# Loading the expert weights of a decoder layer in 2 MB transfers instead of 1 MB ones

## The chip, the cores and the metric

The kernel runs on one core of one Trainium2 chip. The metric is the device time of one execution in microseconds (us). TensorE (PE) multiplies matrices, VectorE (DVE), ScalarE (ACT) and GpSimd (POOL) work on elements, and SyncE (SP) issues nearly all loads; an issued load is moved by the core's 16 DMA engines, which write into the on-chip memory (SBUF, 128 partitions). All numbers are fp32.

## The reference, cut to what matters

The layer has a token mixer (sparse attention beside an RWKV-7 recurrence) and then a mixture of 32 experts over 256 tokens, of which each token uses two. Only the second part bears on the change. Each expert has three weight matrices of 2 MB: gate and up (1024 x 512) and down (512 x 1024).

```python
def body(acc, ew):
    wg, wu, wd, cw = ew
    hdn = jax.nn.silu(xt @ wg) * (xt @ wu)
    return acc + cw[:, None] * (hdn @ wd).astype(f32), None

acc, _ = lax.scan(body, jnp.zeros((T, D), f32), (w_gate, w_up, w_down, combine.T))
```

All 32 experts' weights are read, 192 MB in all, whatever the routing is: for each expert the kernel gathers up to 32 tokens, and a loop at the end, which runs only where an expert has more, takes the rest.

## The kernel before, in words

The first part of the layer takes some 350 us. The experts then go in eight quads of four (`for q in range(NQ)`). For a quad, the tokens are gathered into 128 columns (`fetch`), 32 for each expert. `rows_in` multiplies them with the gate weights and then with the up weights of the four experts: one matmul fills 32 of the 128 rows of a PSUM bank, so four experts run beside each other, and the row blocks `k` of the weights are summed over. `hidden` and `turn_hidden` make silu(gate) x up and transpose it, `rows_down` multiplies with the down weights, `times_gate` and `finish` scale the result and add it to four accumulators in the next quad. The last quad is written out apart (`cols_down`, `parts_down`, `leave`), so that the first 512 columns of the output can leave while the second 512 are computed.

The loads stand in one list, in the order in which they are issued. A weight matrix is cut into two halves of 1 MB: `("eg", e, 0)` and `("eg", e, 1)` are the first and second four row blocks of expert e's gate weights, of which each partition holds a run of 8 KB; `eu` and `ed` are the up and down weights. In the last quad the down weights are cut by columns instead (`ENDS`), and a partition's 1 MB share then comes in four runs of 2 KB. The very first quad's first gate halves come as four `row` loads over four experts.

`pump` issues the next loads of the list as long as the allocator (`Arena`) finds room, in the arena and then in the pool called more, which is the space that an earlier stage has left. `need` gives a loaded tile to the matmuls, and `done` gives its room back and calls `pump`. All this happens when the program is built: the order on SP's queue is the order of the list, and a load into room that has been used waits on the chip for the last matmul that read the tile before it. The loads also take turns on eight completion semaphores, and one that takes a semaphore waits until the load eight places before it, which had the same one, has landed.

In the built program of before, the 1 MB loads of the later quads go round 20 places. A gate group of a quad is 16 matmuls for the first halves of four experts and 16 for the second, each matmul of two instructions (fp32); each half's places are freed after its own 16 matmuls. The names and lines that follow: L288 issues the loads, L1626 is `rows_in`, L1653 `rows_down`, L1660 `cols_down`, L1666 `parts_down`, L1708 `finish`, L1611 the gather.

Of the kernel before, what the change touches and what calls it, by code (L numbers as in the profile page):

```python
# [63 lines left out]
LORD = (0, 1, 2, 3, 4, 5, 6, 7, 8, 9, 10, 12, 13, 15, 11, 14, 17, 16, 18, 23, 19, 20, 21, 22, 24, 28, 25, 27, 26, 29, 30, 31, 32, 33, 34, 35, 36, 37, 38, 44, 40, 39, 41, 42, 51, 45, 43, 47, 48, 52, 50, 46, 49)  # L64
INFO = []
QUADS = NE // 4
ENDS = ((0, 512), (512, 512))
ADAE = 'PPDDDDDDDDDDDDDDDPPPPPPDPPPDPPPDPPPDDDDDDDDDDDDDDDDDDDPPPPPPPPPP'
ADAP = 4
# [88 lines left out]
def layer_kernel(tc, I, out, dbg=None):  # L158
    nc = tc.nc
# [35 lines left out]
    def PS(tag=None):  # L195
        tag = tag or state["tag"]
        return psp.tile([128, 512], F32, name="ps_" + tag, tag=tag, bufs=NB[tag])
# [6 lines left out]
    def add_load(key, shape, parts):  # L204
        loads.append((key, shape, parts))
# [55 lines left out]
    for k in range(4):  # L261
        add_load(("row", k), (1, 2048), [((512 * e, 512 * e + 512), I["expert_w_gate"][0, e].rearrange("(p k) n -> p k n", p=128)
                                          [:, k:k + 1, :]) for e in range(4)])
    for q in range(QUADS):
        for n, name, r in (("eg", "expert_w_gate", 4), ("eu", "expert_w_up", 4), ("ed", "expert_w_down", 2)):
            for i, (c, m) in enumerate(ENDS if n == "ed" and q == QUADS - 1 else ((0, None), (0, None))):
                for e in range(4 * q, 4 * q + 4 if q or n != "eg" or i else 0):
                    w = I[name][0, e].rearrange("(p k) n -> p k n", p=128)
                    if m is None:
                        add_load((n, e, i), (r, 2048 // r), [(None, w[:, r * i:r * i + r, :])])  # L270
                    else:
                        add_load((n, e, i), (4, m), [(None, w[:, :, c:c + m])])
# [20 lines left out]
    def need(key):  # L293
        assert key in W, ("not loaded", key, list(W))
        return W[key]

    def done(key, then=None):
        t = W.pop(key)
        next(a for a in [A] + state["more"] if id(t) in a.live).free(t)
        if then is not None:  # L300
            then()
        pump()
# [90 lines left out]
    for k2 in range(4):  # L393
        ps = PS("rrra"[k2])
# [27 lines left out]
    def mod_bcast(o, row, g0, mul):  # L422

        for g in range(2):
            ps = PS()
            q = 32 * (g0 + g)
            nc.tensor.matmul(ps, ident[:, q:q + 1].to_broadcast([128, 128]), row, start=True, stop=True)
            nc.scalar.mul(o[:, 512 * g:512 * g + 512], ps, mul)
# [69 lines left out]
    def step(it, keep):  # L498

        return after_last(lambda: next(it, "end"), keep)  # L500
# [918 lines left out]
    while todo:  # L1419
# [11 lines left out]
        n = min(turn, key=PRIO.index)  # L1431
# [7 lines left out]
        c = step(it, FORCE)  # L1439
# [53 lines left out]
    for j in range(4):  # L1493
        w = need(("wo", j))
        ws = {}
# [34 lines left out]
    def ME(*shape, dtype=None):  # L1530
        return next(ap for ap in (a.get(*shape, dtype=dtype) for a in [A] + state["more"]) if ap is not None)
# [89 lines left out]

    def rows_in(ps, xg, ws, i):

        for k in range(4):
            for g, w in enumerate(ws):
                nc.tensor.matmul(ps[32 * g:32 * g + 32, :], xg[:, 4 * i + k, 32 * g:32 * g + 32], w[:, k, :],  # L1626
                                 start=(i == 0 and k == 0), stop=(i == 1 and k == 3))

    def row_in(ps, xg, w, k):

        for g in range(4):
            nc.tensor.matmul(ps[32 * g:32 * g + 32, :], xg[:, k, 32 * g:32 * g + 32], w[:, 0, 512 * g:512 * g + 512],  # L1632
                             start=(k == 0), stop=False)

    def hidden(psg, psu, r):

        nc.scalar.activation(thb[0:r], psg[0:r, :], AF.Tanh, scale=0.5)  # L1637
        nc.vector.scalar_tensor_tensor(thb[0:r], thb[0:r], 1.0, psg[0:r, :], op0=OP.add, op1=OP.mult)  # L1638
        nc.vector.scalar_tensor_tensor(hidb[0:r].rearrange("p (j q) -> p q j", j=4), thb[0:r].rearrange("p (q j) -> p q j", j=4),  # L1639
                                       0.5, psu[0:r, :].rearrange("p (q j) -> p q j", j=4), op0=OP.mult, op1=OP.mult)  # L1640

    def turn_hidden(r):
        ps = PS()
        for j in range(4):
            nc.tensor.transpose(ps[:, r * j:r * j + r], hidb[0:r, 128 * j:128 * j + 128], ident[0:r, 0:r])
        nc.scalar.copy(hTb[:, :, 0:r], ps[:, 0:4 * r].rearrange("p (j s) -> p j s", j=4))

    def rows_down(pss, ws, i):

        for c in range(2):  # L1650
            for j in range(2):
                for g, w in enumerate(ws):
                    nc.tensor.matmul(pss[c][32 * g:32 * g + 32, :], hTb[:, 2 * i + j, 32 * g:32 * g + 32],  # L1653
                                     w[:, j, 512 * c:512 * c + 512], start=(i == 0 and j == 0), stop=(i == 1 and j == 1))

    def cols_down(ps, ws):

# [19 lines left out]
    def places(q):  # L1677

        full = [128, 2, 4, CAP]
        es = slice(4 * q, 4 * q + 4)  # L1680
        nc.vector.tensor_tensor(eqb, io1[:, None, None, :].to_broadcast(full), rk[:, :, es][:, :, :, None].to_broadcast(full),
                                op=OP.is_equal)
        for a in range(2):
            nc.vector.tensor_scalar(OHb[:, a], eqb[:, a], rs2[:, a:a + 1], None, op0=OP.mult)

    def fetch(q, k2s=range(4)):
        gather(XGb[q % 2], lambda a: OHb[:, a], 128, k2s)

    def scatter(q):

        nc.gpsimd.tensor_mul(o4b, eqb, comb[:, :, 4 * q:4 * q + 4][:, :, :, None].to_broadcast([128, 2, 4, CAP]))  # L1691
        ps = PS()
        for a in range(2):
            nc.tensor.transpose(ps[:, 128 * a:128 * a + 128], o4b[:, a].rearrange("p g s -> p (g s)"), ident)  # L1694
        nc.scalar.copy(stb[q % 2], ps[:, 0:256].rearrange("p (a t) -> p a t", a=2))

    def begin():

        for a in range(2):
            for c in range(2):  # L1700
                nc.tensor.matmul(acc[2 * a + c].rearrange("p (c k) -> p c k", k=8), ident,  # L1701
                                 h2[:, a, :, 64 * c:64 * c + 64].rearrange("p k c -> p c k"), start=True, stop=False)

    def finish(st, c, r=128, o=None, stop=False):

        o = c if o is None else o
        for a in range(2):
            nc.tensor.matmul(acc[2 * a + c // 512], st[0:r, a, :], Yb[0:r, o:o + 512], start=False, stop=stop)  # L1708
# [12 lines left out]
    def late_rows():  # L1721
# [2 lines left out]

    thb = hidb = hTb = stb = Yb = None
    late = {("eu", 0, 1): late_hidden, ("eu", 1, 1): lambda: (gt2.append(ME(1024)), XGb.append(ME(8, 128))),
            ("eu", 2, 1): late_rows, ("eu", 11, 1): late_tables}
    places(0)
    NQ = QUADS
    for q in range(NQ):  # L1730
        es = range(4 * q, 4 * q + 4)
        psg, psu = PS(), PS()
        for n, ps in (("eg", psg), ("eu", psu)):
            for i in range(2):
                if q == 0 and n == "eg":
                    for k2 in range(2 * i, 2 * i + 2):
                        fetch(0, [k2])
                        for k in () if i else (2 * k2, 2 * k2 + 1):
                            row_in(ps, XGb[0], need(("row", k)), k)
                            done(("row", k))  # L1740
                    if i == 0:
                        continue
                rows_in(ps, XGb[q % 2], [need((n, e, i)) for e in es], i)
                for e in es:
                    done((n, e, i), late.get((n, e, i)))
        hidden(psg, psu, 128)
        if q == 0:
            begin()
            scatter(0)
        if q:  # L1750
            for c in (0, 512):
                finish(stb[(q - 1) % 2], c)
        else:
            mod_bcast(gt2[0], row2, 2, 1.0)
            A.free(row2)
        if q == NQ - 1:
            break
        places(q + 1)
        fetch(q + 1)
        scatter(q + 1)  # L1760
        if q == 2:
            overflow_tables(nc, ovm, PS(), sel, rk, comb, ones, io)
        turn_hidden(128)
        pss = [PS(), PS()]
        for i in range(2):
            rows_down(pss, [need(("ed", e, i)) for e in es], i)
            for e in es:
                done(("ed", e, i))
        for c in range(2):
            times_gate(512 * c, pss[c])  # L1770
# [6 lines left out]
    ps = PS()  # L1777
# [18 lines left out]
    ps = PS()  # L1796
# [4 lines left out]
    ps, p4 = PS(), PS()  # L1801
# [14 lines left out]
    with tc.If(nov > 0):  # L1816
# [3 lines left out]
        with tc.For_i(0, nov, 1) as i:  # L1820
# [15 lines left out]
            for c in (0, 512):  # L1836
                ps = PS()
                parts_down(ps, 0, wts[2][:, :, c:c + 512])
                times_gate(c, ps)
            ps = PS()  # L1840
# [5 lines left out]
            for a in range(2):  # L1846
                for c in range(2):
                    ps = PS()
# [104 lines left out]
```

## Time and profile before

| | us |
|---|---|
| median of 3 runs | 796.88 (796.73 to 797.54) |
| the profiled execution | 798.72 |
| its span, first to last instruction | 796.8 |
| TensorE busy in the span | 676.4 (85%) |
| VectorE, ScalarE, GpSimd busy | 285.3, 167.6, 144.2 |

The span is shown in 40 slices of 19.92 us. Each slice has a digit for the busy share of an engine and of the 16 DMA engines, and the GB/s that these moved. The chain of waits follows the last instruction back to what released it, and so on to the start. A packet is one run of bytes that one DMA engine moves. "SPq" is SP's queue of issues: a load's own time there is the issuing alone, not the transfer.

### The profile page before, as it was taken

To read this page: it belongs to the slowest core of one execution; us is meant where nothing else is said; L and a number is where in the kernel's file an instruction comes from. 1 tells how busy PE (TensorE), PEld (TensorE's weight loads), DVE (VectorE), ACT (ScalarE), POOL (GpSimd) and SP (SyncE) were. 2 spreads that over 40 slices of the span, in tenths; PEclk is the share of its full clock that TensorE was granted. 3 is DMA by queue.
4 is the path that set the end of the run, shared out by engine and by line. 5 is a ranking of instruction groups with operands and counts; after the bars stand their busy time and mean duration, and the time that the engine had idled before them with its cause. 6 is when DMAs were issued, how large, how long until landed. Compare 5 with 4: busy or idle time off the path is not lost.

```text
span 796.8 us, 11470 instructions
## 1 busy us (share of the span) xinstructions
PE 676.4 (85%) x4657; PEld 364.7 (46%) x4657; DVE 285.3 (36%) x665; ACT 167.6 (21%) x347; POOL 144.2 (18%) x176
## 2 busy tenths in 40 slices
PE   5897989799998998889999778878768868878667
PEld 2785657468888877853342312312312312312112
DVE  2577789697336557741210160100100100100001
ACT  2445412144156644321110100100100100000000
POOL 1446744331314117610000000000000000000000
PEclk9899999899999999989999899899999999899889
DMA  9997467443656456779999999999999999999994
GB/s 333 389 308 253 165 221 282 146 154 105 218 208 239 133 178 246 292 257 420 422 421 422 421 420 422 421 420 423 420 421 422 420 421 422 420 421 422 422 392 180
DMA packets 63590, 261.38 MB, mean 328 GB/s; under 512 B 7952, under 2 KB 19216, under 8 KB 38448
## 3 DMA queue, kind: packets, MB, share of 16 engines
q1 hardware_dynamic: 63248, 260.11, 83.4%
q8 instruction: 37, 0.61, 0.3%
q10 hardware_dynamic: 288, 0.52, 0.2%
q14 instruction: 17, 0.14, 0.0%
HBM read 259.57 MB, written 1.05 MB: 327 GB/s over the span
## 4 chain that ended last, share of the span: by engine, by line
DMA 46%; PE 10%; DVE 3%; SPq 1%; issue 1%; POOL 1%; ACT 0%; POOLq 0%; DVEq 0%
DMA arena<-in_expert_w_down_dram 17%; DMA arena<-in_expert_w_gate_dram 13%; DMA arena<-in_expert_w_up_dram 12%; DMA more<-in_expert_w_gate_dram 2%; DMA more<-in_expert_w_up_dram 2%; PE ps_e L1626 2%; DVE split L520 1%; PE ps_e L1611 1%; SPq L288 1%; PE ps_e L1660 1%; PE acc L1701 1%; PE acc L1708 1%; PE ps_e L1653 1%; PE ps_e L1632 0%; PE ps_r L1471 0%
## 5 line engine op out<-in xcount | busy, mean ns | idle before, releaser
L1626 PE MATMUL ps_e<-arena,more 128*32 128x512 f32 x440 | 87.6, 656 | 23.9 <-DMA arena<-in_expert_w_gate_dram 12.0
L1626 PE MATMUL ps_e<-arena 128*32 128x512 f32 x416 | 82.4, 682 | 20.4 <-DMA arena<-in_expert_w_gate_dram 11.7
L1653 PE MATMUL ps_e<-arena 128*32 128x512 f32 x360 | 84.3, 609 | 13.5 <-DMA arena<-in_expert_w_down_dram 9.6
L520 DVE TENSOR_TENSOR split<-arena,split 128x512 fp32r<-128x512 f32 x77 | 70.7, 928 | 45.6 <-ACT split L519 31.8
L1637 ACT ACTIVATE arena<-ps_e 128x512 f32<-128x512 f32 x8 | 4.8, 597 | 244.8 <-PE ps_e L1626 244.8
L1638 DVE SCALAR_TENSOR_TENSOR arena<-arena,ps_e 128x512 f32<-128x512 f32 x8 | 5.5, 688 | 140.2 <-ACT arena L1637 140.2
L1691 POOL TENSOR_TENSOR arena<-arena 128x256 f32<-128x256 f32 x8 | 4.9, 615 | 280.7 <-PE ps_e L1694 279.0
L1670 DVE TENSOR_TENSOR arena<-ps_e,more 128x512 f32<-128x512 f32 (+1 forms) x17 | 11.8, 691 | 122.2 <-PE ps_e L1653 109.1
L519 ACT CAST split<-arena 128x512 fp32r<-128x512 f32 x66 | 45.0, 688 | 48.1 <-PE ps_g L531 30.3
L520 POOL TENSOR_TENSOR split<-arena,split 128x512 fp32r<-128x512 f32 x33 | 47.2, 1431 | 42.6 <-ACT split L519 27.8
L564 PE MATMUL ps_a<-split 128*128 128x256 f32 x360 | 52.1, 304 | 3.1 <-ACT split L476 1.9
L1626 PEld LDWEIGHTS ps_e<-arena,more 128*32 128x32 f32 x440 | 19.4, 118 | 76.3 <-issue 30.9
L564 PEld LDWEIGHTS ps_a<-split 128*128 128x128 f32 x360 | 47.9, 205 | 12.1 <-issue 6.5
L1626 PEld LDWEIGHTS ps_e<-arena 128*32 128x32 f32 x416 | 17.8, 122 | 74.0 <-issue 35.8
L517 POOL TENSOR_SCALAR split<-arena 128x512 fp32r<-128x512 f32 x44 | 36.9, 842 | 70.2 <-PE ps_g L531 18.7
L1653 PEld LDWEIGHTS ps_e<-arena 128*32 128x32 f32 x360 | 19.6, 110 | 64.3 <-issue 31.2
L530 PE MATMUL ps_g<-split 128*128 128x256 f32 x128 | 39.1, 306 | 0.0
L532 PE MATMUL ps_g<-split 128*128 128x256 f32 x128 | 36.9, 289 | 2.0 <-POOL split L520 2.0
L1639 DVE SCALAR_TENSOR_TENSOR arena<-arena,ps_e 128x512 f32<-128x512 f32 x8 | 8.2, 1029 | 82.5 <-PE ps_e L1626 82.5
L531 PE MATMUL ps_g<-split 128*128 128x256 f32 x128 | 36.8, 288 | 0.0
L1611 PEld LDWEIGHTS ps_e<-arena,more 128*128 128x128 f32 x256 | 30.7, 195 | 13.2 <-issue 8.2
L532 PE MATMUL ps_a<-split 128*128 128x256 f32 (+1 forms) x96 | 30.4, 317 | 6.2 <-DVE split L520 6.2
(378 smaller groups left out, 1192.5 us busy)
## 6 DMA issues: line engine op xcount, KB each, us to landing
arena<-in_expert_w_gate_dram SPq DMA_DIRECT2D x54, 1024.0 KB, 19.8
arena<-in_expert_w_up_dram SPq DMA_DIRECT2D x53, 1024.0 KB, 19.8
arena<-in_expert_w_down_dram SPq DMA_DIRECT2D x53, 1024.0 KB, 19.8
arena<-in_w_in_dram SPq DMA_DIRECT2D x18, 1024.0 KB, 7.8
arena<-in_ada_w_dram SPq DMA_DIRECT2D x16, 1024.0 KB, 6.1
more<-in_expert_w_up_dram SPq DMA_DIRECT2D x11, 1024.0 KB, 19.8
more<-in_expert_w_down_dram SPq DMA_DIRECT2D x11, 1024.0 KB, 19.8
arena<-in_ada_w_dram SPq DMA_DIRECT2D x16, 512.0 KB, 10.9
```

Of the source, the lines that this page charges most:

```text
L517: nc.gpsimd.tensor_scalar(h, w, 1.0, 0.0, op0=OP.mult, op1=OP.add)
L519: nc.scalar.copy(h, w)
L520: (nc.gpsimd if p[1] == "P" else nc.vector).tensor_sub(l, w, h.bitcast(F32))
L530: nc.tensor.matmul(ps, l[0], r[0], start=start, stop=False)
L531: nc.tensor.matmul(ps, l[0], r[1], start=False, stop=False)
L532: nc.tensor.matmul(ps, l[1], r[0], start=False, stop=stop)
L564: nc.tensor.matmul(p, a[:, kk, :], b[:, 4 * hf + kk, :], start=(i == 0 and kk == KORD[0]), stop=(i == 2 and kk == KORD[-1]))
L1611: nc.tensor.matmul(ps[:, n * kk:n * kk + n], h2[:, a, 2 * k2 + kk, :], oh(a), start=(a == 0), stop=(a == 1))
L1626: nc.tensor.matmul(ps[32 * g:32 * g + 32, :], xg[:, 4 * i + k, 32 * g:32 * g + 32], w[:, k, :], start=(i == 0 and k == 0), stop=(i == 1 an ...
L1639: nc.vector.scalar_tensor_tensor(hidb[0:r].rearrange("p (j q) -> p q j", j=4), thb[0:r].rearrange("p (q j) -> p q j", j=4), 0.5, psu[0:r, ...
L1653: nc.tensor.matmul(pss[c][32 * g:32 * g + 32, :], hTb[:, 2 * i + j, 32 * g:32 * g + 32], w[:, j, 512 * c:512 * c + 512], start=(i == 0 and ...
L1670: nc.vector.tensor_mul(Yb[0:r, c:c + 512], ps[0:r], gt2[0][0:r, g:g + 512])
```

## The change

From the third quad on, that is from expert 8, a weight matrix comes in one load of 2 MB: the four row blocks twice over, 16 KB in one run for each partition. The up and down weights of the last quad keep their 1 MB pieces, the down weights their column halves. `rows_in` and `rows_down` take as many row blocks as the tile has, so that one call covers what two covered, and the loops over the two halves run once. The room for the overflow tables is taken when the one up tile of expert 11 is freed.

```diff
--- before.py
+++ after.py
@@ -64,6 +64,7 @@
 LORD = (0, 1, 2, 3, 4, 5, 6, 7, 8, 9, 10, 12, 13, 15, 11, 14, 17, 16, 18, 23, 19, 20, 21, 22, 24, 28, 25, 27, 26, 29, 30, 31, 32, 33, 34, 35, 36, 37, 38, 44, 40, 39, 41, 42, 51, 45, 43, 47, 48, 52, 50, 46, 49)
 INFO = []
 QUADS = NE // 4
+WHOLE = 2
 ENDS = ((0, 512), (512, 512))
 ADAE = 'PPDDDDDDDDDDDDDDDPPPPPPDPPPDPPPDPPPDDDDDDDDDDDDDDDDDDDPPPPPPPPPP'
 ADAP = 4
@@ -261,9 +262,18 @@
     for k in range(4):
         add_load(("row", k), (1, 2048), [((512 * e, 512 * e + 512), I["expert_w_gate"][0, e].rearrange("(p k) n -> p k n", p=128)
                                           [:, k:k + 1, :]) for e in range(4)])
+    def whole(n, q):
+
+        return q >= WHOLE and not (n != "eg" and q == QUADS - 1)
+
     for q in range(QUADS):
         for n, name, r in (("eg", "expert_w_gate", 4), ("eu", "expert_w_up", 4), ("ed", "expert_w_down", 2)):
             for i, (c, m) in enumerate(ENDS if n == "ed" and q == QUADS - 1 else ((0, None), (0, None))):
+                if whole(n, q):
+                    if i == 0:
+                        for e in range(4 * q, 4 * q + 4):
+                            add_load((n, e, 0), (2 * r, 2048 // r), [(None, I[name][0, e].rearrange("(p k) n -> p k n", p=128))])
+                    continue
                 for e in range(4 * q, 4 * q + 4 if q or n != "eg" or i else 0):
                     w = I[name][0, e].rearrange("(p k) n -> p k n", p=128)
                     if m is None:
@@ -1621,10 +1631,10 @@
 
     def rows_in(ps, xg, ws, i):
 
-        for k in range(4):
+        for k in range(4 * i, 4 * i + ws[0].shape[1]):
             for g, w in enumerate(ws):
-                nc.tensor.matmul(ps[32 * g:32 * g + 32, :], xg[:, 4 * i + k, 32 * g:32 * g + 32], w[:, k, :],
-                                 start=(i == 0 and k == 0), stop=(i == 1 and k == 3))
+                nc.tensor.matmul(ps[32 * g:32 * g + 32, :], xg[:, k, 32 * g:32 * g + 32], w[:, k - 4 * i, :],
+                                 start=(k == 0), stop=(k == 7))
 
     def row_in(ps, xg, w, k):
 
@@ -1648,10 +1658,10 @@
     def rows_down(pss, ws, i):
 
         for c in range(2):
-            for j in range(2):
+            for j in range(2 * i, 2 * i + ws[0].shape[1]):
                 for g, w in enumerate(ws):
-                    nc.tensor.matmul(pss[c][32 * g:32 * g + 32, :], hTb[:, 2 * i + j, 32 * g:32 * g + 32],
-                                     w[:, j, 512 * c:512 * c + 512], start=(i == 0 and j == 0), stop=(i == 1 and j == 1))
+                    nc.tensor.matmul(pss[c][32 * g:32 * g + 32, :], hTb[:, j, 32 * g:32 * g + 32],
+                                     w[:, j - 2 * i, 512 * c:512 * c + 512], start=(j == 0), stop=(j == 3))
 
     def cols_down(ps, ws):
 
@@ -1724,14 +1734,14 @@
 
     thb = hidb = hTb = stb = Yb = None
     late = {("eu", 0, 1): late_hidden, ("eu", 1, 1): lambda: (gt2.append(ME(1024)), XGb.append(ME(8, 128))),
-            ("eu", 2, 1): late_rows, ("eu", 11, 1): late_tables}
+            ("eu", 2, 1): late_rows, ("eu", 11, 0 if whole("eu", 2) else 1): late_tables}
     places(0)
     NQ = QUADS
     for q in range(NQ):
         es = range(4 * q, 4 * q + 4)
         psg, psu = PS(), PS()
         for n, ps in (("eg", psg), ("eu", psu)):
-            for i in range(2):
+            for i in range(1 if whole(n, q) else 2):
                 if q == 0 and n == "eg":
                     for k2 in range(2 * i, 2 * i + 2):
                         fetch(0, [k2])
@@ -1762,7 +1772,7 @@
             overflow_tables(nc, ovm, PS(), sel, rk, comb, ones, io)
         turn_hidden(128)
         pss = [PS(), PS()]
-        for i in range(2):
+        for i in range(1 if whole("ed", q) else 2):
             rows_down(pss, [need(("ed", e, i)) for e in es], i)
             for e in es:
                 done(("ed", e, i))
```

On SP's queue, at the change from the second quad to the third (L288 before is L298 now):

```order
L288 DMA arena<-in_expert_w_down_dram 128x2048 x6
L288 DMA arena<-in_expert_w_gate_dram 128x2048 x8
L288 DMA arena<-in_expert_w_up_dram 128x2048 x3
L288 DMA more<-in_expert_w_up_dram 128x2048 x3
L288 DMA arena<-in_expert_w_up_dram 128x2048 x2
L288 DMA arena<-in_expert_w_down_dram 128x2048 x8
```

Now:

```order
L298 DMA arena<-in_expert_w_down_dram 128x2048 x6
L298 DMA arena<-in_expert_w_gate_dram 128x4096 x4
L298 DMA more<-in_expert_w_up_dram 128x4096
L298 DMA arena<-in_expert_w_up_dram 128x4096 x3
L298 DMA arena<-in_expert_w_down_dram 128x4096 x4
L298 DMA more<-in_expert_w_gate_dram 128x4096
```

Eight gate loads of 1 MB become four of 2 MB, and the up and down loads behind them likewise; the tiles' places differ, one of four being in more. In all, 128 loads of 1 MB become 64 of 2 MB. In the built program these go round eight places of 2 MB, two sets of four.

On TensorE, at the third quad's gate matmuls (L1626 before is L1636 now, L1708 is L1718, L1611 is L1621, L1694 is L1704):

```order
L1708 MATMUL acc_3382<-arena 128x512
L1708 MATMUL acc_3384<-arena 128x512
L1626 MATMUL ps_e<-arena 32x512
L1708 MATMUL acc_3383<-arena 128x512
L1708 MATMUL acc_3385<-arena 128x512
L1626 MATMUL ps_e<-arena 32x512 x32
L1611 MATMUL ps_e<-arena,more 128x128 x11
L1626 MATMUL ps_e<-arena 32x512
L1611 MATMUL ps_e<-arena,more 128x128 x5
L1694 MATMUL ps_e<-arena 128x128 x2
```

Now:

```order
L1718 MATMUL acc_3382<-arena 128x512
L1718 MATMUL acc_3384<-arena 128x512
L1718 MATMUL acc_3383<-arena 128x512
L1718 MATMUL acc_3385<-arena 128x512
L1636 MATMUL ps_e<-arena 32x512 x32
L1636 MATMUL ps_e<-more,arena 32x512
L1621 MATMUL ps_e<-arena,more 128x128 x13
L1636 MATMUL ps_e<-arena 32x512
L1621 MATMUL ps_e<-arena,more 128x128 x3
L1704 MATMUL ps_e<-arena 128x128 x2
```

The first gate matmul stood among the four `finish` matmuls and waited for the first gate half; now the four stand together, and the 32 gate matmuls of the quad follow in one piece. The count of matmuls is as before. `rows_down` runs over all four row blocks for the first 512 columns and then for the second, where it ran over two blocks for both. VectorE's, ScalarE's and GpSimd's orders are the same in both programs.

On SP's queue, the last quad's loads:

```order
L288 DMA arena<-in_expert_w_gate_dram 128x2048 x8
L288 DMA arena<-in_expert_w_up_dram 128x2048 x3
L288 DMA more<-in_expert_w_up_dram 128x2048 x3
L288 DMA arena<-in_expert_w_up_dram 128x2048 x2
L288 DMA arena<-in_expert_w_down_dram 128x4x512 x8
```

Now:

```order
L298 DMA more<-in_expert_w_gate_dram 128x4096
L298 DMA arena<-in_expert_w_gate_dram 128x4096 x3
L298 DMA arena<-in_expert_w_up_dram 128x2048 x2
L298 DMA more<-in_expert_w_up_dram 128x2048
L298 DMA arena<-in_expert_w_up_dram 128x2048 x5
L298 DMA arena<-in_expert_w_down_dram 128x4x512 x3
L298 DMA more<-in_expert_w_down_dram 128x4x512 x2
L298 DMA arena<-in_expert_w_down_dram 128x4x512 x3
```

The first two rows now are the 2 MB gate loads; behind them stand eight up loads and eight down column halves of 1 MB in both programs, in other places.

## Rows read from the trace of the kernel before

**Rows 1.** The page's slices: DMA busy share, GB/s moved, and the packets by size

```profile
DMA  9997467443656456779999999999999999999994
GB/s 333 389 308 253 165 221 282 146 154 105 218 208 239 133 178 246 292 257 420 422 421 422 421 420 422 421 420 423 420 421 422 420 421 422 420 421 422 422 392 180
DMA packets 63590, 261.38 MB, mean 328 GB/s; under 512 B 7952, under 2 KB 19216, under 8 KB 38448
```

**Rows 2.** The page's chain that ended last: shares of the span by engine, then by line

```profile
DMA 46%; PE 10%; DVE 3%; SPq 1%; issue 1%; POOL 1%; ACT 0%; POOLq 0%; DVEq 0%
DMA arena<-in_expert_w_down_dram 17%; DMA arena<-in_expert_w_gate_dram 13%; DMA arena<-in_expert_w_up_dram 12%; DMA more<-in_expert_w_gate_dram 2%; DMA more<-in_expert_w_up_dram 2%; PE ps_e L1626 2%; DVE split L520 1%; PE ps_e L1611 1%; SPq L288 1%; PE ps_e L1660 1%; PE acc L1701 1%; PE acc L1708 1%; PE ps_e L1653 1%; PE ps_e L1632 0%; PE ps_r L1471 0%
```

**Rows 3.** Chain in order of time, from 713 us: start us, us, what

```profile
713.16 19.78 DMA arena<-in_expert_w_gate_dram
733.01 19.81 DMA arena<-in_expert_w_up_dram
752.88 9.20 SPq L288
762.17 13.97 DMA arena<-in_expert_w_down_dram
776.18 5.14 PE ps_e L1660 x26
...
784.07 3.25 PE ps_e L1660 x21
...
788.61 3.65 PE acc L1708 x8
```

**Rows 4.** Stretches: columns as the first row names them, the last two are DMA share, GB/s

```profile
core 0: us, PE busy (x) PEld busy (x) DVE busy (x) ACT busy (x) POOL busy (x), PEclk, DMA share, GB/s
...
520.00:740.00 220.00, 174.36 (x854) 50.88 (x854) 17.13 (x32) 9.75 (x22) 2.83 (x4) 0.96 1.01 421
764.00:778.00 14.00, 9.36 (x50) 2.67 (x54) 1.02 (x1) 0.86 (x2) 0.00 (x0) 0.80 1.05 387
```

**Rows 5.** The page's DMA issues: form xcount, KB each, us from issue to landing

```profile
arena<-in_expert_w_gate_dram SPq DMA_DIRECT2D x54, 1024.0 KB, 19.8
arena<-in_expert_w_up_dram SPq DMA_DIRECT2D x53, 1024.0 KB, 19.8
```

**Rows 6.** Line 288 (all loads): issue to landing, shortest, median, longest

```profile
DMA to landing us min/median/max: 2.8/19.8/21.4
```

**Rows 7.** Waits of SP's queue: us in total, times, longest us

```profile
SPq L288 <- DMA arena<-in_expert_w_gate_dram: 93.9, 45, 2.1
SPq L288 <- DMA arena<-in_expert_w_up_dram: 86.7, 42, 2.2
...
SPq L288 <- PE ps_e L1653: 15.2, 13, 9.4
...
SPq L288 <- PE ps_e L1626: 11.3, 18, 4.5
```

**Rows 8.** Order of time on SP's queue, 406 to 449 us: start us, us, what

```profile
406.91 19.29 SPq L288 DMA_DIRECT2D arena<-in_expert_w_gate_dram  x8
428.36 5.30 SPq L288 DMA_DIRECT2D arena<-in_expert_w_up_dram  x3
435.81 5.28 SPq L288 DMA_DIRECT2D more<-in_expert_w_up_dram  x3
```

**Rows 9.** Order of time on TensorE, 729 to 752 us: start us, us, what [idle before]

```profile
729.08 1.98 PE L1708 MATMUL acc<-arena 128*128 128x512 f32 x4
...
735.46 3.63 PE L1626 MATMUL ps_e<-arena,more 128*32 128x512 f32 x28 [0.53 <-DMA arena<-in_expert_w_gate_dram]
740.43 1.05 PE L1626 MATMUL ps_e<-arena,more 128*32 128x512 f32 x2 [1.34 <-DMA arena<-in_expert_w_gate_dram]
742.92 1.05 PE L1626 MATMUL ps_e<-arena,more 128*32 128x512 f32 x2 [1.44 <-DMA arena<-in_expert_w_gate_dram]
745.41 6.02 PE L1626 MATMUL ps_e<-arena,more 128*32 128x512 f32 x30 [1.44 <-DMA arena<-in_expert_w_gate_dram]
```

## The prediction

> **What bounds the kernel now.** I read the page's slices first: from the 19th on, some 360 us into the span, the DMA engines are busy 9 tenths or more and move 420 to 423 GB/s slice after slice, to the 38th [rows 1]. Before that the digits are mostly lower and the time goes to the token mixer. Then the chain of waits: 46% of the span on it is DMA and 10% TensorE, and the DMA is nearly all expert weights [rows 2]. In order of time it shows blocks of eight 1 MB loads of about 19.8 us each, one behind the other, until the last down pieces land at 776.18 us, then the last quad's matmuls and the output [rows 3]. So the second half of the kernel is a stream at a steady rate: its length is bytes by rate, and it is followed by a tail of some 20 us.
>
> The stream is not starved. A load takes 19.8 us from issue to landing, where one takes 2.49 us of the engines (below), so eight are in flight [rows 5]. SP waits longest in total for earlier loads, in steps of at most 2.2 us, that is for one of the eight semaphores; its waits for matmuls to free room sum to 15.2 and 11.3 us over the whole span [rows 7], and in the stretch from 520 to 740 us the engines stand at a share of 1.01 in spite of them [rows 4]. TensorE is busy 174.36 of those 220 us, some of it at a lower clock (0.96 on the mean) [rows 4]; it waits for the loads.
>
> So the change matters through the rate of the stream, through the risk that bigger places starve it, and through the tail.
>
> **The rate.** Two stretches are pure in the size of their runs. From 520 to 740 us every partition's share is a run of 8 KB, and the rate is 421 GB/s; from 764 to 778 us the last quad's down pieces come in runs of 2 KB, and it is 387 GB/s [rows 4]. 1 MB (1,048,576 bytes) takes 2.491 us in the first and 2.709 us in the second. Each of 16 engines moves 64 KB of it, in 8 runs or in 32. The difference, 218 ns over 24 more runs, is 9.1 ns a run; without runs' cost 1 MB would take 2.491 - 8 x 0.0091 = 2.418 us, which is 434 GB/s. That a run of 8 KB is one packet is borne out by the count: 63,590 - 38,448 = 25,142 packets are of 8 KB or more [rows 1]; 180 expert loads and 16 others with such runs make 196 x 128 = 25,088.
>
> With 16 KB runs an engine has 4 runs per MB: 2.418 + 4 x 0.0091 = 2.455 us, 427 GB/s, 36.5 ns less per MB. 128 MB change their form (gate of quads 3 to 8, up and down of quads 3 to 7: 48 + 40 + 40). That is 128 x 0.0365 = 4.7 us. No row of before has a run over 8 KB, so both ends: if 8 runs' whole cost went, 128 x 0.073 = 9.3 us would be saved; if a 16 KB run were cut in pieces of 4 KB, an engine would have 16 per MB, 8 more than now, and 9.3 us would be lost. I take the value on the line through the two measured sizes, as 8 KB, its nearer point, is measured in a full stream.
>
> The Trainium skill ("DMA: Bandwidth & Descriptors", section "Why a DMA increments its semaphore by 16 and not by 1") says that one descriptor moves one contiguous run, and tells of cutting only for rows beyond 64 KiB; by that 16 KB stays whole. No run here shows it yet.
>
> 64 issues fewer on SP's queue, and the room for the overflow tables taken one `done` sooner: SP waits anyway and VectorE's order is the same, so 0. If a load had a fixed cost of its own beside its runs, half of these costs would go too; but the fixed part can't be large: eight loads in flight keep the share at 1.01.
>
> The Trainium skill (the same title, section "Anatomy of one DMA") gives a fixed 2 us for each load issued through GpSimd. By that alone 64 loads fewer would save 128 us. The 2.491 us per 1 MB load leave no place for it: beside seven others it is hidden, and it stays out of the sum.
>
> **The room.** Before, 1 MB loads go round 20 places; now 2 MB loads round 8, in two sets of four, and a set is freed only when all its 32 matmuls have run. When a group of four lands, the next group is already issued, 4 x 4.91 = 19.6 us of stream. How long do 32 matmuls need? A half's 16 (32 instructions, of which the trace holds 30) took 6.02 us where TensorE had sat idle in pieces of 1.4 us; another half ran 28 of its 32 in 3.63 us, which is 4.1 us a half and the fast pace [rows 9]. So 6.0 + 4.1 = 10.1 us, 12 if the second half runs at the slow pace as well. The four `finish` matmuls (1.98 us for four instructions, twice) [rows 9] stand ahead of the gate group and run while it lands. The next set is thus issued 7.6 to 9.5 us before the stream needs it, and the shortest load took 2.8 us from issue to landing [rows 6]. Cost 0; cover some 5 us.
>
> The tightest place is the entry to this order. There, expert 11's up load is the first that waits for a whole gate group (the last matmuls of experts 8 to 11), and only three up loads of 2 MB, 14.7 us, are in front of it: 14.7 - 10.1 - 2.8 = 1.8 us to spare, nothing at 12 us. Before, SP's issue of this stretch was paced by landings and gaps of a few us, 426.2 to 428.36 and 433.66 to 435.81 [rows 8]. I take 0, with one gap of up to 4 us as the bad end.
>
> **The tail.** The last eight up loads and the column halves keep size and order. The one difference is that the last gate group's 32 matmuls all come after its last landing: 10.1 us, where the first four up pieces land 4 x 2.49 = 10.0 us later and their 16 matmuls (6 us) have until 19.9 us. Finished at 16.1: cover 3.8 us. If that cover went, the excess would show one to one. SP's one long issue, 9.20 us at 752.88 [rows 3], belongs to the 2 KB pieces and stays. From the last landings on, the chain is as now, so 0.
>
> **Sum.** -4.7 + 0 + 0 + 0 = -4.7 us on the profiled execution: 798.72 (span 796.8 and 1.9 around it) to 794.0. That one lies 1.8 above the median of the runs; the median goes from 796.88 to 792.2.
>
> **Rivals.** (B) *Less than the line says.* Only part of the 9.1 ns is paid per run at large sizes, the rest belongs to short runs. For it: two points make any line. Against it: the cost-free rate that follows, 434 GB/s, is above every slice of the page [rows 1] but near them. With a third of the cost, -1.6 us: 795.3. The Trainium skill ("DMA: Bandwidth & Descriptors", "Why small descriptors are slow") has about 3 cycles of a 32-byte bus per packet, 259 cycles instead of 256 for 8 KB; going to 16 KB would then save 0.6% of 319 us, 1.9 us. The rows give three times that.
>
> (C) *No change in rate.* The 16 KB runs are cut in two on the way, or something else than packets holds 421 GB/s. For it: no row excludes it. Against it: 2 KB runs are slower in the same stream. Time 796.9; the packet count would stay at 63,590.
>
> (D) *Slower: starvation.* The 16 MB in eight places, freed in whole sets, are less elastic than 20 MB in twenty. With pieces arriving every 4.9 us and not every 2.5 us, TensorE sits idle longer and may run whole groups at half the fast pace: 4 x 4.1 = 16.4 us, and more if a `finish` or gather matmul stands behind a landing. From 16.8 us (19.6 - 2.8) on each excess us is an idle us of stream, in each of 16 groups. With 1 us, and 4 at the entry, 20 - 4.7 = +15: 812. For it: TensorE's share of 79% has little slack. Against it: the order has finish and gather ahead of the last landing.
>
> (E) *Slower: cut to 4 KB*, from the bound above: +9.3, 806.
>
> **Numbers.** About 0.2% (1.6 us) is what a measurement of this kernel can tell from no change. Forecast 0.58, B 0.13, C 0.14, D 0.10, E 0.05. B sits at the edge: half of it counts as no change. Faster 0.66, within 0.2% 0.19, slower 0.15. The forecast's own range is 790.8 to 793.8 (-6 to -3). For 8 in 10, the range takes in B and C, up to 797.6, and on the side of the full 9.3 us half the way, 789.5; D and E, 0.15, stay out.
>
> **What would show it.** Right: the slices from the 23rd on at 426 to 428 GB/s and still without a dip; 8,192 packets fewer, about 55,400; blocks of 8 MB at about 19.6 us in the chain in place of 19.8; the last down landings near 771.5 us, the time from there to the end as now. SP's waits for matmuls will be longer in the list and cost nothing. Wrong: 421 GB/s (C), a packet count that rises (E), a slice under 9 tenths of DMA between 420 and 760 us or a dip near 460 us (D).

## The result, and the profile after

The changed kernel takes 792.21 us (median of 7 runs, 790.66 to 794.46), the kernel before 797.24 (7 runs, 796.73 to 797.73): a ratio of 0.9937, 95% interval 0.9923 to 0.995, or 5.0 us less (4.0 to 6.1). Measured twice more it was 0.9956 (0.9944 to 0.9969) and 0.9951 (0.9937 to 0.9966). The forecast was 792.2.

The page of the changed kernel, the slices and the packets, against [rows 1]:

```profile
DMA  9997467543666456779999999999999999999995
GB/s 334 388 307 264 162 225 269 166 155 100 223 213 241 134 182 245 273 261 392 422 421 429 428 425 428 431 426 426 428 432 423 427 430 427 426 428 427 421 394 204
DMA packets 54372, 261.36 MB, mean 331 GB/s; under 512 B 6928, under 2 KB 18192, under 8 KB 37424
```

From the 22nd slice to the 38th the stream moves 421 to 432 GB/s where it moved 420 to 423. The packets are 9,218 fewer, and the classes show which: those of 8 KB or more fall from 25,142 to 16,948, that is by 8,194; the 1,024 others are under 512 B. Four stretches, with the columns of [rows 4] (the last three are PEclk, the granted share of TensorE's clock, the DMA share and GB/s):

```profile
520.00:740.00 220.00, 157.28 (x862) 48.51 (x866) 17.26 (x32) 9.75 (x22) 2.82 (x4) 0.86 1.01 427
758.00:772.00 14.00, 10.22 (x63) 2.95 (x64) 1.03 (x1) 0.86 (x2) 0.00 (x0) 0.86 1.05 387
440.00:450.00 10.00, 7.03 (x44) 1.78 (x48) 0.00 (x0) 0.00 (x0) 0.00 (x0) 0.60 1.00 424
450.00:460.00 10.00, 9.03 (x62) 5.13 (x54) 4.30 (x14) 2.47 (x6) 0.62 (x1) 1.00 1.02 433
```

In the same 220 us the rate is 427 GB/s for 421, and it is 387 still where the column pieces with 2 KB runs land. At the entry, from 440 to 460 us, the engines stay at a share of 1.00 and more. TensorE's granted clock is 0.86 on the mean for 0.96, and 0.60 from 440 to 450 us, where it begins a group after an idle time.

The waits of SP's queue, against [rows 7]:

```profile
SPq L298 <- PE ps_e L1636: 201.4, 19, 23.4
SPq L298 <- PE ps_e L1663: 95.3, 13, 18.4
...
SPq L298 <- DMA arena<-in_expert_w_gate_dram: 19.3, 7, 4.6
```

SP waits for matmuls 297 us in total instead of 26.5. A reader of this list alone would say that the stream is now held up by TensorE. The share of 1.01 says that it isn't: SP waits ahead of time. The same in order of time on SP's queue, against [rows 8]:

```profile
406.02 7.78 SPq L298 DMA_DIRECT2D arena<-in_expert_w_gate_dram  x4
419.48 0.33 SPq L298 DMA_DIRECT2D more<-in_expert_w_up_dram  x1
426.20 25.77 SPq L298 DMA_DIRECT2D arena<-in_expert_w_up_dram  x3
452.03 1.85 SPq L298 DMA_DIRECT2D arena<-in_expert_w_down_dram  x4
```

and on TensorE, against [rows 9]:

```profile
438.08 1.92 PE L1636 MATMUL ps_e<-arena 128*32 128x512 f32 x2 [3.85 <-DMA arena<-in_expert_w_gate_dram]
442.97 9.06 PE L1636 MATMUL ps_e<-arena 128*32 128x512 f32 x57 [2.98 <-DMA arena<-in_expert_w_gate_dram]
```

The last of expert 8 to 11's gate loads lands at 442.97 us. Three of the 32 gate matmuls, the first ones of the experts that had landed before, have run by then (one of them is the row at 438.08). The other 29, of whose 58 instructions this row holds 57, take 9.06 us, and the third up load of the row at 426.20 (expert 11's) is issued as they end, close to 451.6. The three up loads ahead of it end 3 x 4.9 = 14.7 us after 442.97, at 457.7. So the tightest load is issued 6 us before the stream comes to it.

The end of the chain of waits, against [rows 3]:

```profile
699.43 8.52 PE ps_e L1636 x56
...
709.24 29.31 DMA arena<-in_expert_w_gate_dram
738.57 19.86 DMA arena<-in_expert_w_up_dram
758.48 4.63 PE ps_e L1636 x25
763.11 14.25 DMA arena<-in_expert_w_down_dram
777.40 3.19 PE ps_e L1670 x19
...
781.88 3.65 PE acc L1718 x8
```

Where the 2 MB loads come, their blocks no longer stand one behind the other in this chain. It goes from a set's matmuls to a load that they let go, and from its issue to its landing: 29.31 us, which is 12 MB of stream at 427 GB/s. Four loads of 2 MB are 19.6 us of it, so the set was issued some 10 us before the engines came to it.

The profiled spans differ by 7.0 us (796.8 to 789.8), which divides as follows. On TensorE, expert 11's gate weights have landed before at 445.72 us:

```profile
445.72 6.51 PE L1626 MATMUL ps_e<-arena 128*32 128x512 f32 x28 [1.44 <-DMA arena<-in_expert_w_gate_dram]
```

Now they have landed at 442.97: 2.75 us, of which the change can have given 8 x 0.0365 = 0.3. The rest is scatter: the same landing comes between 442.85 and 446.25 us in six other profiles that run the same program up to the 2 MB loads: the changed kernel's two repeats, and variants below that have its places. From there to the landing of the last gate weights, 120 MB further on, it is 299.69 us before (to 745.41, [rows 9]) and 295.60 now (to 738.57): 4.1 us, where 120 x 0.0365 = 4.4 were forecast; the two repeats have 295.25 and 295.19, so 4.4 and 4.5. From there on nothing changes: the first columns' last piece lands 30.8 us later in both (776.18, [rows 3], and 769.32), and the end comes 20.6 and 20.5 us after it.

### The profile page after: what moved, and what is told of

It is laid out like the page before. It is cut to its first block, busy times and chain, and to the rows that moved or that the text cites. A ratio compares the mean times of both kernels' runs of the same rounds, so it can differ in the third digit from the quotient of the medians.

```text
span 789.8 us, 11330 instructions
## 1 busy us (share of the span) xinstructions
PE 646.8 (82%) x4657; PEld 358.3 (45%) x4657; DVE 286.4 (36%) x665; ACT 167.5 (21%) x347; POOL 144.3 (18%) x176
## 4 chain that ended last, share of the span: by engine, by line
DMA 42%; PE 14%; DVE 3%; issue 1%; SPq 1%; POOL 1%; ACT 0%; POOLq 0%; DVEq 0%
DMA arena<-in_expert_w_gate_dram 16%; DMA arena<-in_expert_w_up_dram 14%; DMA arena<-in_expert_w_down_dram 12%; PE ps_e L1636 8%; PE ps_e L1663 2%; DVE split L530 2%; SPq L298 1%; PE ps_e L1621 1%; PE acc L1711 0%; PE ps_e L1642 0%; PE acc L1718 0%; PE ps_e L1670 0%; POOL split L530 0%; PE ps_r L1481 0%; POOL split L527 0%
## 5 line engine op out<-in xcount | busy, mean ns | idle before, releaser
L1636 PE MATMUL ps_e<-arena 128*32 128x512 f32 x424 | 81.9, 709 | 34.5 <-DMA arena<-in_expert_w_gate_dram 20.6
L1636 PE MATMUL ps_e<-arena,more 128*32 128x512 f32 x448 | 84.6, 704 | 30.7 <-DMA arena<-in_expert_w_gate_dram 17.5
L1663 PE MATMUL ps_e<-arena 128*32 128x512 f32 x376 | 78.7, 663 | 21.6 <-DMA arena<-in_expert_w_down_dram 18.4
L1636 PEld LDWEIGHTS ps_e<-arena,more 128*32 128x32 f32 x448 | 19.2, 127 | 89.0 <-issue 45.5
L1636 PEld LDWEIGHTS ps_e<-arena 128*32 128x32 f32 x424 | 18.4, 127 | 90.6 <-issue 44.5
L1663 PEld LDWEIGHTS ps_e<-arena 128*32 128x32 f32 x376 | 19.1, 119 | 69.3 <-issue 37.0
L540 PE MATMUL ps_g<-split 128*128 128x256 f32 x128 | 38.4, 300 | 0.0
L542 PE MATMUL ps_g<-split 128*128 128x256 f32 x128 | 36.3, 284 | 2.0 <-POOL split L530 2.0
L1621 PEld LDWEIGHTS ps_e<-arena,more 128*128 128x128 f32 x256 | 30.9, 196 | 12.9 <-issue 8.2
L541 PE MATMUL ps_g<-split 128*128 128x256 f32 x128 | 36.2, 282 | 0.0
```

The costliest lines, as they stand in the source:

```text
L540: nc.tensor.matmul(ps, l[0], r[0], start=start, stop=False)
L541: nc.tensor.matmul(ps, l[0], r[1], start=False, stop=False)
L542: nc.tensor.matmul(ps, l[1], r[0], start=False, stop=stop)
L1621: nc.tensor.matmul(ps[:, n * kk:n * kk + n], h2[:, a, 2 * k2 + kk, :], oh(a), start=(a == 0), stop=(a == 1))
L1663: nc.tensor.matmul(pss[c][32 * g:32 * g + 32, :], hTb[:, j, 32 * g:32 * g + 32], w[:, j - 2 * i, 512 * c:512 * c + 512], start=(j == 0), s ...
```

## The experiments

The theory: each run of bytes costs an engine 9.1 ns beside its bytes, so the rate follows the run's length. The rivals: each load has a cost, whatever its runs; and the grouping of matmuls and places moves the time by itself, for better or worse. The first four experiments are compared with the same 23 runs of the kernel before, median 797.58 us.

**Two loads for each tile.** The tiles, places and matmuls of the changed kernel, with loads of 1 MB and runs of 8 KB as before.

```diff
-add_load((n, e, 0), (2 * r, 2048 // r), [(None, I[name][0, e].rearrange("(p k) n -> p k n", p=128))])
+w = I[name][0, e].rearrange("(p k) n -> p k n", p=128)
+add_load((n, e, 0), (2 * r, 2048 // r), [(lambda t, o=o, r=r: t[:, o:o + r, :], w[:, o:o + r, :]) for o in (0, r)])
...
-dst = t if sl is None else t[:, :, sl[0]:sl[1]]
+dst = t if sl is None else sl(t) if callable(sl) else t[:, :, sl[0]:sl[1]]
```

Expected: 

> The 2 MB tiles, their eight places, the order of the matmuls and all waits for room stay as in the changed kernel, but each tile is filled by two loads of 1 MB (its first and second row blocks), so runs are 8 KB again and there are 128 loads. If the gain is the longer run or the smaller count of loads, the stream from 520 to 740 us falls back to 421 GB/s and the time to that of before, 796.9 to 797.2 us. If the gain came from the grouping (one row of 32 matmuls, places freed in sets), the rate doesn't matter and the time stays at 792.

Measured: 797.5 us, ratio to before 0.9995 (0.998 to 1.001). Its packets on the page, and the stretch from 520 to 740 us:

```profile
DMA packets 63589, 261.37 MB, mean 328 GB/s; under 512 B 7952, under 2 KB 19216, under 8 KB 38448
```

```profile
520.00:740.00 220.00, 157.58 (x854) 48.05 (x854) 17.27 (x32) 9.76 (x22) 2.83 (x4) 0.87 1.01 421
```

421 GB/s at the clock (0.87) and in the grouping of the changed kernel: the grouping neither gives nor costs anything that these runs can tell, and TensorE's lower clock doesn't either.

**One load, two runs of 8 KB.**

```diff
-add_load((n, e, 0), (2 * r, 2048 // r), [(None, I[name][0, e].rearrange("(p k) n -> p k n", p=128))])
+add_load((n, e, 0), (2 * r, 2048 // r), [(lambda t: t.rearrange("p (h k) n -> p h (k n)", h=2),
+                      I[name][0, e].rearrange("(h p k) n -> p h (k n)", h=2, p=128))])
```

Expected: 

> One load of 2 MB for each tile as in the changed kernel (64 loads), but from rows in the memory that lie in two pieces, so that each partition's share is two runs of 8 KB. (Rows of weights and tokens are paired wrongly by this, so the sums differ.) By the cost per run (9.1 ns, 8 runs per MB and engine): 421 GB/s, 797 us, 8,192 packets more than in the changed kernel. By a cost per load, whatever its runs: 427 GB/s, 792 us. A mixture shows as a rate between.

Measured: 797.23 us, 0.9994 (0.998 to 1.0008).

```profile
DMA packets 62564, 261.36 MB, mean 328 GB/s; under 512 B 6928, under 2 KB 18192, under 8 KB 37424
```

```profile
520.00:740.00 220.00, 158.67 (x860) 48.65 (x858) 18.20 (x35) 10.84 (x25) 3.45 (x5) 0.85 1.01 421
```

The loads are halved and the rate is that of before. Against the run above, 1,024 of the 1,025 packets fewer are under 512 B: 16 for each of the 64 loads that went. They don't show in the rate, 421 with them and without. So the cost is the run's, and a load's own cost doesn't show here to within 1 GB/s.

**One load, four runs of 4 KB** (`h=4` in the lines above).

Expected: 

> The same with four runs of 4 KB for each partition (again rows are paired wrongly). By the cost per run the 1 MB takes 2.418 + 16 x 0.0091 = 2.564 us, 409 GB/s, and the time is 792.2 + 128 x (2.564 - 2.455) = 806 us. By a cost per load alone: 427 GB/s, 792 us. If the cost per run is no straight line in the count of runs, the rate is off 409 by more than 2 GB/s.

Measured: 805.73 us, 1.0103 (1.0083 to 1.0124).

```profile
DMA packets 78948, 261.36 MB, mean 325 GB/s; under 512 B 6928, under 2 KB 18192, under 8 KB 70192
```

```profile
520.00:740.00 220.00, 154.07 (x845) 46.82 (x846) 17.07 (x33) 10.18 (x24) 3.05 (x5) 0.86 1.03 409
```

409 GB/s, as the line through 2 and 8 KB gives. Four sizes of run now lie on one line: 387, 409, 421 and 427 GB/s at 2, 4, 8 and 16 KB, or 2.709, 2.564, 2.491 and 2.456 us per MB with 32, 16, 8 and 4 runs on each engine. The steps are 9.1, 9.1 and 8.8 ns a run (1 GB/s more or less at 16 KB moves the last by 1.4 ns). This also rules out, for this stream, that the cost belongs to short runs alone.

**Loads of 1 MB with runs of 16 KB**, by halves of the partitions.

```diff
+w = I[name][0, e].rearrange("(p k) n -> p k n", p=128)
+add_load((n, e, 0), (2 * r, 2048 // r), [(lambda t, o=o: t[o:o + 64], w[o:o + 64]) for o in (0, 64)])
```

Expected: 

> Each 2 MB tile filled by two loads of 1 MB, one for partitions 0 to 63 and one for 64 to 127, each with runs of 16 KB: the long runs without the smaller count of loads (128). By the cost per run: 427 GB/s and 792 us. By a cost per load: 421 GB/s and 797 us. If half the partitions cannot take the full rate, it is far below both, which would show as a rate under 400 GB/s and a time over 810 us.

Measured: 1090.29 us, 1.3592 (1.353 to 1.3654).

```profile
520.00:740.00 220.00, 102.85 (x450) 29.50 (x454) 9.83 (x21) 5.53 (x13) 1.23 (x2) 0.68 1.01 220
```

This is the third of the expected cases: 220 GB/s at a full DMA share. The engines are occupied all the time and move half. It says nothing on the two theories, as the halves hide the difference; the three runs above had settled it.

**From the second quad on**, with the changed kernel again beside it. Of that, expected: 

> The changed kernel once more, beside the two variants on the same chip: 792 us, 5 us under the kernel before, 427 GB/s from 520 to 740 us.

Measured: 792.99 us, 0.9956 (0.9944 to 0.9969). The variant:

```diff
-WHOLE = 2
+WHOLE = 1
```

Expected: 

> 2 MB loads from the second quad on already (24 loads of 1 MB more become 12 of 2 MB). By the cost per run 24 x 0.0365 = 0.9 us less than the changed kernel, 791.3 us, if the room bears it. By the rival that sets of places starve the stream: TensorE still works off what came early in the second quad, so its sets come free late there; a gap of 2 us or more, and a slice under 9 tenths of DMA between 360 and 420 us, would make it 793 us or more.

Measured: 800.57 us, 1.005 (1.0036 to 1.0065): 7.6 us over the changed kernel. Stretches of 10 us, of this variant and then of the changed kernel:

```profile
360.00:370.00 10.00, 10.00 (x95) 3.07 (x97) 1.27 (x4) 1.40 (x3) 0.00 (x0) 1.00 0.67 254
370.00:380.00 10.00, 10.00 (x53) 5.76 (x46) 3.22 (x8) 2.50 (x6) 0.62 (x1) 1.00 1.01 429
380.00:390.00 10.00, 9.01 (x77) 2.90 (x76) 1.97 (x4) 1.44 (x4) 0.62 (x1) 1.00 0.62 238
390.00:400.00 10.00, 10.00 (x69) 3.01 (x67) 0.00 (x0) 0.00 (x0) 0.00 (x0) 1.00 0.94 400
```

```profile
360.00:370.00 10.00, 10.00 (x96) 2.90 (x94) 0.97 (x3) 1.41 (x3) 0.00 (x0) 1.00 1.00 406
...
380.00:390.00 10.00, 9.01 (x86) 2.76 (x88) 1.81 (x3) 1.14 (x4) 0.46 (x1) 1.00 1.01 419
```

The stream itself is fast (429 from 370 to 380 us), but it has two holes, at 254 and 238 GB/s. At 427 GB/s they are 4.1 and 4.4 us of nothing, and with 0.6 us from 390 to 400 that is 9.1. The changed kernel's 406 GB/s from 360 to 370 makes 0.4. The difference of 8.7, less the 0.9 that 24 MB gain, is 7.8, against 7.6 measured. SP's queue shows what the holes are:

```profile
354.60 1.41 SPq L298 DMA_DIRECT2D arena<-in_expert_w_down_dram  x2
363.83 4.75 SPq L298 DMA_DIRECT2D arena<-in_expert_w_gate_dram  x4
388.57 0.33 SPq L298 DMA_DIRECT2D more<-in_expert_w_up_dram  x1
389.00 10.54 SPq L298 DMA_DIRECT2D arena<-in_expert_w_up_dram  x3
```

And what it waits for between 340 and 430 us:

```profile
SPq L298 <- PE ps_e L1663: 20.0, 1, 20.0
```

The last two down loads of the first quad are issued by 356.0, the next load, the first of 2 MB, at 363.83; then the row of four is issued by 368.6, and nothing until 388.57, where the first quad's down matmuls (L1663), for which the queue has waited 20.0 us, have freed the next place. Four loads of 2 MB are 19.6 us of stream. TensorE was busy all of 360 to 380 us (10.00 of 10.00 in both stretches): the first quads' weights have come early, it works them off, and its sets come free late. So the rival holds here, with gaps far longer than the 2 us from which it was to show.

**The same places, loads of 1 MB** (`WHOLE = 1` in the first experiment's kernel).

Expected: 

> The 2 MB places from the second quad on, as in the variant that was 3.5 us slower than before, but each filled by two loads of 1 MB (8 KB runs). If that variant's loss is the room (a place is free only when all of a set's matmuls have run), the stream has the same gaps between 360 and 400 us and the time is some 8 us over the kernel before, 805. If it is the 2 MB loads that wait longer for their turn, the gaps close and the time is 797.

Measured: 802.63 us, 1.0066 (1.0047 to 1.0085), 5.3 us over before by the ratio (4 to 7), 4.5 by the medians (798.1 before). Two stretches and SP's queue:

```profile
360.00:370.00 10.00, 10.00 (x96) 2.86 (x88) 0.80 (x2) 1.27 (x3) 0.00 (x0) 1.00 0.96 355
...
380.00:390.00 10.00, 9.01 (x77) 2.60 (x80) 1.81 (x3) 0.96 (x3) 0.29 (x1) 1.00 0.64 225
```

```profile
358.61 11.51 SPq L299 DMA_DIRECT2D arena<-in_expert_w_gate_dram  x8
384.72 3.71 SPq L299 DMA_DIRECT2D more<-in_expert_w_up_dram  x2
```

The second hole stays as deep (225 GB/s, 4.7 us at 421) and is the places' doing: it ends 4 us earlier, at 384.72, but the gate loads ahead of it also came 5 us earlier. The first hole is mostly gone (355 GB/s, 1.6 us): a load of 1 MB can go as soon as its own half of a place is free, one of 2 MB needs both, and the first gate load is issued at 358.61 us, not at 363.83. The first experiment's kernel, the same but for `WHOLE`, has 386 GB/s from 360 to 370 us, 0.8 us of nothing. Less that, the two holes make 5.5 us, against the 5.3 or 4.5 measured. So one of the variant's holes comes with the places, whatever the size of the load, and most of the other came with that size.

**The last up weights whole.** In pieces only the last down weights.

```diff
-return q >= WHOLE and not (n != "eg" and q == QUADS - 1)
+return q >= WHOLE and not (n == "ed" and q == QUADS - 1)
```

Expected: 

> The last quad's up weights in 2 MB loads as well, only its down weights in pieces. The stream gains 8 x 0.0365 = 0.3 us. But the 32 up matmuls (10.1 us, with the transpose behind them some 3 us more) then all come after the last up landing, where the first four down pieces land 4 x 2.71 = 10.8 us later: the end is 13 - 10.8 = 2 us later, 794 us. If the pieces of the last up weights don't matter, 791.9 us.

Measured: 791.43 us, 0.993 (0.9917 to 0.9943), on the chip on which the changed kernel had 792.99. Repeated, with both side by side:

Expected of the changed kernel: 

> The changed kernel, to stand beside the next run on one chip: 792.5 us.

 Of the variant: 

> The variant with the last up weights whole, repeated: its median was 1.6 us under the changed kernel's, but its profiled span 0.7 us over. If it is really faster, its median is again 1 us or more under that of the changed kernel beside it; if the first was scatter, they lie within 1 us.

Measured: 793.1 and 790.73 us; 0.9951 (0.9937 to 0.9966) and 0.9921 (0.9908 to 0.9935). So it is faster than both kernels, by 1.6 and 2.4 us than the changed one. The first pair's runs overlap (790.48 to 793.4 us against 792.57 to 794.34); the second pair's don't (790.27 to 791.25 against 791.66 to 794.18). My expectation had the wrong sign. On TensorE, the variant and then the changed kernel beside it:

```profile
757.69 8.41 PE L1636 MATMUL ps_e<-arena,more 128*32 128x512 f32 x58 [3.85 <-DMA arena<-in_expert_w_up_dram]
...
768.61 0.62 PE L1670 MATMUL ps_e<-arena 128*32 128x512 f32 x2 [0.51 <-ACT arena L1656]
...
776.53 0.62 PE L1670 MATMUL ps_e<-arena 128*32 128x512 f32 x1 [0.48 <-DMA arena<-in_expert_w_down_dram]
```

```profile
758.53 6.48 PE L1636 MATMUL ps_e<-arena,more 128*32 128x512 f32 x26 [1.51 <-DMA arena<-in_expert_w_up_dram]
...
767.52 1.06 PE L1670 MATMUL ps_e<-arena 128*32 128x512 f32 x6 [0.51 <-ACT arena L1656]
769.37 0.62 PE L1670 MATMUL ps_e<-more,arena 128*32 128x512 f32 x1 [0.79 <-DMA more<-in_expert_w_down_dram]
```

Of the variant's 32 up matmuls 29 (58 instructions) are left at the last landing, and they need 8.41 us, where I had 10.1 for all 32. The first columns' matmuls start at 768.61; in the changed kernel the first three experts' start at 767.52, and the fourth's waits for its down piece until 769.37. So what the pieces are to save is waited out a step later. In both the end then hangs on the last down piece, at 776.53 and 777.42. Of the profiled spans' difference of 1.2 us, 0.5 stands before the last up weights, 0.3 is their stream (8 x 0.0365) and 0.3 comes after the last landing. The medians differ by about 1 us more, which I can't place; the changed kernel's profiled execution is the fastest of its six (791.66 us, median 793.1).

## Why the prediction was right, point by point

**The rate** was right: 2.455 us per MB or 427 GB/s forecast, 427 GB/s measured. The 9.1 ns a run held in four sizes. The Trainium skill ("DMA: Bandwidth & Descriptors", "Why a DMA increments its semaphore by 16 and not by 1") has one descriptor for one contiguous run. The packets of 8 KB or more agree: 8,194 fewer, so the runs of 16 KB stay whole.

**The count of packets** was off by 1,024. The forecast left out the 16 small ones of each load. By the same section of the Trainium skill each of the engines that a load uses posts its own completion. The trace agrees: 16 for each of 64 loads is what went.

**The rivals.** B (part of the cost) is out by the 4 KB and 16 KB runs. The estimate beside it from a figure of the Trainium skill ("DMA: Bandwidth & Descriptors", "Why small descriptors are slow"), 1.9 us, doesn't agree: the traces have 4.1 to 4.5 us in 120 MB. The forecast's 4.7 us are 2.5 times that estimate, not three times, as the prediction has it. C (no change in rate) and E (cut to 4 KB) are out by the packets.

**The room** was costed at 0, and was 0: the kernel with these places and 8 KB runs is as fast as the one before. The working was too tight. It let all 32 matmuls run after the last landing, in 10.1 us; 29 are left then, and the next load was issued after 8.7 us (442.97 to 451.6). So 3.2 us beyond the 2.8 of the shortest load were to spare at the entry, not 1.8, and later sets were issued some 10 us ahead, not 7.6 to 9.5. The times that it took from [rows 9] were misread too: by the order of the landings the 6.02 us hold the last 13 gate matmuls and two of the up group, not a half's 16. SP's waits for earlier loads, put at 2.2 us at most, went to 3.7 at loads of down weights; nothing hangs on that. D's mechanism is real, and lies one quad away: from the second quad on places of 2 MB leave two holes of 4 us. D's trigger was a TensorE at half its fast pace. Its granted clock did fall, from 0.96 to 0.86 between 520 and 740 us, and cost nothing there; what empties the stream in the variant is that TensorE is still behind with the first quads.

**The tail** kept its length, 20.6 and 20.5 us after the last piece of the first columns. It was forecast that the last gate group's matmuls end just as the fourth up piece lands; TensorE waited 1.44 us for that piece in this profile, and 0.27 us in another of the changed kernel. That cutting the last up weights into pieces of 1 MB saves 2 us, which I then worked out in the same way for the variant, was wrong: the variant without the cut is faster.

**The signs.** The slices scatter more than forecast, 423 to 432 GB/s and not 426 to 428, around the mean of 427. Blocks of 19.6 us, forecast for the chain, aren't in it, as the sets' matmuls now stand between; the rate they were to show is in the stretch. The last landing of the first columns came at 769.32 us for a forecast of 771.5: the 2.4 us of scatter ahead of expert 11's landing account for that.

**The sum**: -4.7 us against -5.0 in the medians (and -4.1 and -4.1 in the two repeats), of which the traces show 4.1 to 4.5 in 120 of the 128 MB. The profiled execution took 791.66 us for a forecast of 794.0, by the same 2.4 us, which are scatter. That the median fell on the forecast to a hundredth is luck, with runs that scatter over 3.8 us. By its own chances, with half of B, faster had 0.645 and no change 0.205, not 0.66 and 0.19.

## What to carry to other kernels

In this stream, which keeps the DMA engines full, time is bytes plus runs, and what gave the gain is the length of the run, not the size of the load: 2 MB loads with 8 KB runs gave nothing. Count the contiguous runs of each partition, measure two sizes in pure stretches, and the line through them gives a third, here one beyond both. Bigger places are the price, and what they cost was decided here at one spot, where the stream first has to wait for a whole set to come free: work out the time between that landing and the end of the queue, and compare it with the matmuls that have to run. A list of waits that grows tenfold means nothing as long as the waiter is early; the DMA share of the stretch tells which it is. The share doesn't tell the rate: the loads of half the partitions kept it at 1.01 and moved 220 GB/s.

## What the runs showed of the hardware

Loads that fill 64 of the 128 partitions, by turns the lower and the upper half, ran at 220 GB/s with the engines' mean busy share at 1.01, against 427 for 128 partitions with the same runs. Sixteen packets under 512 B go with each load, and in a full stream they cost nothing that shows (421 GB/s with 128 loads and with 64). In this full stream no fixed time of a load shows (64 loads of 2 MB and 128 of 1 MB, both with 8 KB runs, at 421 GB/s); what shows beside the bytes is 9 ns for each run on its engine, at 2, 4, 8 and 16 KB.
